# Layer 0's experts ordered on the chip by their token counts: eight with 128 slots, eight with 64 in pairs

## The chip, the core and the metric

One NeuronCore of a Trainium2 chip runs the whole program. The metric is device time of one execution in microseconds (us), lower is better. The engines are PE (matmuls, with its weight loads shown as PEld), DVE (vector), ACT (scalar), POOL and SP. SP computes nothing here: it issues the loads from device memory. A "q" behind an engine's name (SPq, ACTq) is its queue of instructions that do not compute.

## The reference, cut to what matters

Two layers; each ends in a mixture of experts over its tokens, 512 in layer 0 (256 of context, 256 latent) and 256 in layer 1. Every token goes to two of 16 experts, and each expert is a SwiGLU of width 512:

```python
probs = softmax(h @ w_router); ...
e_idx = g_idx[:, None] * EXPERTS_PER_GROUP + loc      # two experts of one group
...
return (jax.nn.silu(xblk @ w_gate[e]) * (xblk @ w_up[e])) @ w_down[e]
...
return jax.ops.segment_sum(y * weight, token)
```

`w_gate` and `w_up` are 1024 x 512 and `w_down` 512 x 1024, all float32, so one expert's weights are 6 pieces of 1.05 MB, 6.29 MB in all, and the 16 experts of a layer 100.7 MB. With the reference's inputs, expert 0 of layer 0 has 121 tokens; the other fifteen have, from most to fewest, 106, 91, 85, 81, 67, 66, 58 and then 58, 48, 47, 45, 43, 43, 38, 27.

## The kernel before

The mixture of layer 0 is the part `if full:` of `tail`. Routing leaves, for each expert, the places of its tokens in 128 slots (`place_tiles`, `indices`): `gix`, by which POOL gathers rows of the tokens from device memory (`gather`), and `six`, by which it scatters the result rows (`scatter`). `cnt` holds the counts and their maximum. Every engine loads that maximum and branches on it (`past_slots`): if some expert had more tokens than slots, `overflow` would run. With these inputs it doesn't.

Then the loop takes the experts 0 to 15 in turn. For each: eight transposes of the gathered rows (`expert_rows`, into `xh` and `xl`), the up and gate products (`expert_wide_up`, four pieces of weights), transposes of the activations (`expert_acts`), and the down product (`expert_wide_down`, two pieces). Each piece is split into a high part (`whi`, ACT, L233) and a low part (`wlo`, DVE, L234), and each product is three matmuls of 128 x 128 on 512 columns (L245 to L247). The up products of an expert stand ahead of the down product of the one before. The last two experts are not scattered; they are added through a matrix (`back_matrix`).

The pieces come through a ring of 12 tiles (`wtile`), of which the last two experts take two for their results. SP issues the loads in one written order (`Ahead.todo`); each waits until its tile has been read. A tile is free once both of its splits are done. Behind the experts' pieces SP issues six pieces of `w_ada` (L256), the scattered rows (`y<-yd`, L1742) and two more pieces of `w_ada`. PE multiplies the first `w_ada` pieces (L268), and then `combine` adds the rows (L1761).

Layer 1's mixture has 64 slots for each expert: `expert_half_up` (L1575) and `pair_down` (L1603) multiply the unsplit float32 weights, with two 64-column halves of PE side by side. The change doesn't touch it; its rows are of use below.

Of the kernel before, what the change touches and what calls it, by code (L numbers as in the profile page):

```python
# [23 lines left out]
D = 1024  # L24
# [52 lines left out]
def kernel(es, tc, A, out, dbg=None):  # L77
# [882 lines left out]

    class Ahead:


        def __init__(self, l):
            self.l = l
            self.done = {}

            up = lambda e: [(e, p) for p in range(4)]
            if l:
                down = lambda e: [(e + i, p) for p in (4, 5) for i in (0, 1)]  # L970
                self.todo = up(0) + up(1)
                for e in range(2, 16, 2):
                    self.todo += up(e) + down(e - 2) + up(e + 1)
                self.todo += down(14)
            else:
                down = lambda e: [(e, p) for p in (4, 5)]
                self.todo = up(0)
                for e in range(1, 16):
                    self.todo += up(e) + down(e - 1)
                self.todo += down(15)  # L980

        def fetch(self, n):
            for _ in range(n):
                f = self.todo.pop(0)
                self.done[f] = expert_piece(self.l, *f)
# [10 lines left out]
    def tail(l, mp, mgp, mg, side, other):  # L996
# [18 lines left out]
        with ExitStack() as ms, ExitStack() as ps_:  # L1015
# [13 lines left out]
            cnt = mo.tile([1, 17], I32, name="cnt")  # L1029
            mcol = mo.tile([128, 16 * len(rr) + 8], F32, name="mcol")  # L1030
            if full:
# [3 lines left out]
                gix = mo.tile([128, 16], U32, name="gix")  # L1035
                six = mo.tile([128, 16], U32, name="six")
# [5 lines left out]
            with ExitStack() as rs_:  # L1042
# [3 lines left out]
                if full:  # L1046
                    n2 = xg[0]
                    m34 = rp.tile([128, 2, 2, D], F32, name="m34")
                    cc = rp.tile([128, 3, 16], F32, name="cc")
                    rnb = rp.tile([128, nt, 16], BF16, name="rnb")  # L1050
# [61 lines left out]
                def tile_done(t):  # L1112
# [46 lines left out]
                    if t % 2 == 0:  # L1159
                        return  # L1160
                    weights.append(route(rp, lgs[0], t, nt, br, wts, comb, ohb, rnk, rnb if full else None, rhs, utr, one,
                                         cnt, (rows_a, rows_b) if t == nt - 1 else None))
                    if full:
                        nonlocal placed
                        placed = place_tiles(rp, (t - 1, t), cap, iot, rnb, rhs, cc, None if t < nt - 1 else
                                    lambda g: indices(rp, cc, gix, six, g))
                    if full and t == nt - 1:
                        weigh(placed)

# [22 lines left out]
                def past_slots(overflow_):  # L1192
                    mx = nc.values_load(cnt[0:1, 16:17], min_val=0, max_val=128 * nt)
# [33 lines left out]
            if full:  # L1227
                for e in range(2):
                    gather(l, xg[e], gix[:, e:e + 1], nt)
                past_slots(lambda: overflow(l, side, nt, cap, rnk, rhs, cnt))  # L1230
# [3 lines left out]
                def rows_of(e):  # L1234

                    nonlocal g
                    if e < NE:
                        rows[e] = expert_rows(ex, xg[e % 2])
                    if e + 2 < NE:
                        g = gather(l, xg[e % 2], gix[:, e + 2:e + 3], nt)  # L1240

                def acts_of(e):
                    if e >= 0:
                        acts[e] = expert_acts(ex, acts[e])

                for e in range(NE + 1):
                    if e == 0:
                        rows_of(0)
                    if e < NE:

                        with tc.issue_after(placed.ins) if e == 0 else nullcontext():
                            acts[e] = expert_wide_up(ex, e, rows.pop(e), load, lambda: acts_of(e - 1))
                    if e == 0:
                        rows_of(1)
                    if e == NE // 2:
                        m5 = [None, ex.tile([128, D], F32, name="m5")]
                        SY.dma_start(m5[1], m_dram[l][1, 5 * D:].partition_broadcast(128))
                        with tc.issue_after(g.ins):
                            back = [back_matrix(ex, i, nt, rnk, comb) for i in (NE - 2, NE - 1)]
                    if e:  # L1260
                        if e == NE:
                            acts_of(e - 1)
                        MT, ws = back[e - 1 - (NE - 2)] if e > NE - 2 else (None, None)
                        y = expert_wide_down(l, ex, e - 1, acts.pop(e - 1), six[:, e - 1:e], load, lambda: rows_of(e + 1), ws)
# [21 lines left out]
    def route(rp, lg, t1, NT_, br, wts, comb, ohb, rnk, rnb, rhs, utr, one, cnt, meanwhile):  # L1286
# [64 lines left out]
        if last:  # L1351
# [4 lines left out]
            V.tensor_copy(cf[:, 0:16], pc[0:1])  # L1356
            V.tensor_reduce(cf[:, 16:17], cf[:, 0:16], AX.X, ALU.max)
            V.tensor_copy(cnt, cf)
# [12 lines left out]
        return weights  # L1371

# [23 lines left out]
    def indices(mo, cc, gix, six, g):  # L1396

        e = slice(8 * g, 8 * g + 8)
        I = mo.tile([128, 8], F32, name="I", bufs=2)
        J = mo.tile([128, 8], F32, name="J", bufs=2)  # L1400
        K = mo.tile([128, 8], F32, name="K", bufs=2)

        V.scalar_tensor_tensor(I, cc[:, 1, e], 128.0, cc[:, 0, e], ALU.mult, ALU.add)
        V.tensor_scalar(J, cc[:, 2, e], 0.5, BIG, ALU.is_lt, ALU.mult)
        V.tensor_tensor(gix[:, e], I, J, ALU.add)
        V.tensor_scalar(K, J, C[:, CPID:CPID + 1], -1.0, ALU.mult, ALU.add)
        V.scalar_tensor_tensor(I, I, 2.0, cc[:, 2, e], ALU.mult, ALU.add)
        return V.tensor_tensor(six[:, e], I, K, ALU.add)
# [42 lines left out]
    def expert_piece(l, e, p):  # L1451

        if l == 0:
            r = wtile([128, 4, 512])
            if p < 4:

                loads.append(SY.dma_start(r, A[("w_gate", "w_up")[p % 2]][l, e].rearrange("(p k) n -> p k n", k=8)[
                    :, 4 * (p // 2):4 * (p // 2) + 4]))
            else:

                loads.append(SY.dma_start(r.rearrange("p (k c) n -> p k (c n)", c=2),
# [353 lines left out]
```

## Time and profile before

| | |
|---|---|
| median of three runs | 1747.82 us (1746.91 to 1748.83) |
| the profiled execution | 1750.19 us, its span 1748.4 us |
| PE busy | 1667.5 us, 95% of the span |
| DVE, ACT busy | 1034.2 us (59%), 805.2 us (46%) |
| moved by transfers | 380.03 MB, 217 GB/s on average |

Times in the trace are us from the span's start. The mixture of layer 0 lies between about 731 and 1036 us, that of layer 1 between about 1510 and 1745 us.

### The profile page before, as it was taken

Reading aid. Unit: us, or ns where it says so; the run is one execution under the profiler, and the core shown is the slowest. Engines: PE = TensorE matmul, PEld = TensorE weight load, DVE = VectorE, ACT = ScalarE, POOL = GpSimd, SP = SyncE. Lnnn points to the kernel's source line nnn. Section 1 sums busy time; section 2 is a strip of 40 time slices with the busy share of each in tenths; the row PEclk is TensorE's granted clock in tenths of the full one; section 3 lists DMA queues with packets and bytes.
Section 4 is the critical chain, followed back from the end, with each engine's and each line's share of the span. In section 5 each row is a group of like instructions: output and inputs, shape, how many; then the busy total and the mean of one; then the engine's idle time right before and its main releaser. Section 6 shows DMA issues by size and latency. Waiting matters only on the chain. (4 is left out here: it accounts for less than half of the span.)

```text
span 1748.4 us, 24188 instructions
## 1 busy us (share of the span) xinstructions
PE 1667.5 (95%) x8944; PEld 1231.4 (70%) x8945; DVE 1034.2 (59%) x1905; ACT 805.2 (46%) x1343; POOL 304.0 (17%) x322
## 2 busy tenths in 40 slices
PE   7999999999999999699999999999999999799998
PEld 4657878886677888488877766878887887443333
DVE  4328673557776345699978866578548865411101
ACT  3313432356577341288878755434446874211100
POOL 0003130412210221011131001133313202100000
PEclk9999999999999999799999999999999998899999
DMA  9895434233121473799999875422434348799996
GB/s 290 294 314 192 121 124 162 75 97 88 34 73 38 108 261 124 285 419 414 395 349 356 328 296 161 117 82 84 144 97 122 96 109 295 276 414 413 412 381 252
DMA packets 198448, 380.03 MB, mean 217 GB/s; under 512 B 33446, under 2 KB 130214, under 8 KB 176432
## 3 DMA queue, kind: packets, MB, share of 16 engines
q1 hardware_dynamic: 186384, 361.19, 58.3%
q10 hardware_dynamic: 7616, 9.43, 1.7%
q0 software_dynamic: 4320, 7.75, 1.2%
q8 instruction: 75, 1.23, 0.3%
q14 instruction: 53, 0.43, 0.1%
HBM read 370.50 MB, written 17.72 MB: 222 GB/s over the span
## 5 line engine op out<-in xcount | busy, mean ns | idle before, releaser
L234 DVE TENSOR_TENSOR wlo<-wraw,whi 128x1024 fp32r<-128x1024 f32 (+2 forms) x368 | 439.6, 1220 | 174.5 <-ACT whi L233 166.4
L233 ACT CAST whi<-wraw 128x1024 fp32r<-128x1024 f32 (+2 forms) x368 | 367.1, 1024 | 141.4 <-PE psg L246 59.4
L245 PE MATMUL psg<-hTh,whi 128*128 128x512 f32 (+1 forms) x576 | 205.6, 359 | 0.0
L246 PE MATMUL psg<-hTl,whi 128*128 128x512 f32 (+1 forms) x576 | 204.7, 356 | 0.0
L247 PE MATMUL psg<-hTh,wlo 128*128 128x512 f32 (+1 forms) x576 | 203.8, 356 | 0.0
L245 PE MATMUL psg<-whi,hTh 128*128 128x512 f32 (+1 forms) x392 | 147.8, 381 | 2.2 <-ACT hTh L379 2.1
L246 PE MATMUL psg<-wlo,hTh 128*128 128x512 f32 (+1 forms) x392 | 147.8, 378 | 0.1
L247 PE MATMUL psg<-whi,hTl 128*128 128x512 f32 (+1 forms) x392 | 146.8, 378 | 0.0
L245 PEld LDWEIGHTS psg<-hTh,whi 128*128 128x128 f32 x576 | 108.4, 188 | 20.7 <-issue 6.8
L247 PEld LDWEIGHTS psg<-hTh,wlo 128*128 128x128 f32 x576 | 108.3, 188 | 17.1 <-issue 4.4
L246 PEld LDWEIGHTS psg<-hTl,whi 128*128 128x128 f32 x576 | 108.6, 188 | 16.3 <-issue 4.0
L1575 PE MATMUL psg<-wraw,xT 128*64 128x512 f32 x512 | 113.4, 595 | 2.9 <-PEq L1194 2.8
L246 PE MATMUL psg<-wlo,xh 128*128 128x512 f32 x256 | 103.0, 402 | 2.7 <-DVE wlo L234 2.5
L245 PE MATMUL psg<-whi,xh 128*128 128x512 f32 x256 | 102.3, 400 | 1.4 <-ACT xh L1484 1.4
L247 PE MATMUL psg<-whi,xl 128*128 128x512 f32 x256 | 100.8, 395 | 0.0
L1575 PEld LDWEIGHTS psg<-wraw,xT 128*64 128x64 f32 x512 | 35.8, 137 | 74.0 <-issue 71.4
L245 PEld LDWEIGHTS psg<-whi,hTh 128*128 128x128 f32 x392 | 74.0, 189 | 19.3 <-ACT hTh L379 3.8
L247 PEld LDWEIGHTS psg<-whi,hTl 128*128 128x128 f32 x392 | 73.8, 189 | 15.3 <-issue 1.0
L246 PEld LDWEIGHTS psg<-wlo,hTh 128*128 128x128 f32 x392 | 74.1, 189 | 13.9 <-issue 0.5
L593 ACT ACTIVATE P<-P,smx 128x512 f32<-128x512 f32 (+1 forms) x96 | 62.3, 649 | 22.1 <-DVE smx L592 19.7
L842 POOL TENSOR_TENSOR mg<-mg,gates 128x512 f32<-128x512 f32 (+1 forms) x32 | 38.1, 1199 | 171.7 <-DVE gates L841 104.0
L1580 ACT ACTIVATE act<-psg 128x256 f32<-128x256 f32 x16 | 6.2, 384 | 130.8 <-PE psg L1575 107.3
(410 smaller groups left out, 3249.0 us busy)
## 6 DMA issues: line engine op xcount, KB each, us to landing
wraw<-in_w_down_dram SPq DMA_DIRECT2D x64, 1024.0 KB
wraw<-in_w_ada_dram SPq DMA_DIRECT2D x40, 1024.0 KB
wraw<-in_w_in_dram SPq DMA_DIRECT2D x144, 256.0 KB
wraw<-in_w_gate_dram SPq DMA_DIRECT2D x32, 1024.0 KB
wraw<-in_w_up_dram SPq DMA_DIRECT2D x32, 1024.0 KB
wraw<-in_w_gate_dram SPq DMA_DIRECT2D x64, 512.0 KB
wraw<-in_w_up_dram SPq DMA_DIRECT2D x64, 512.0 KB
wraw<-in_w_in_dram SPq DMA_DIRECT2D x24, 1024.0 KB
```

The source lines that it names most:

```text
L233: S.copy(hi[:, :, 0:n], r[:, 2 * j:2 * j + 2, 0:n])
L234: splits[0] = V.tensor_tensor(lo[:, :, 0:n], r[:, 2 * j:2 * j + 2, 0:n], hi.bitcast(F32)[:, :, 0:n], ALU.subtract)
L245: PE.matmul(ps, ah, bh, start=start, stop=False)
L246: PE.matmul(ps, ah, bl, start=False, stop=False)
L247: return PE.matmul(ps, al, bh, start=False, stop=stop)
L593: S.activation(flat, flat, AF.Exp, scale=-1.0, bias=m[:, 0:1], accum_out=m[:, 2:3])
L842: G.tensor_tensor(dst, dst, sg[:, i], ALU.add)
L1575: PE.matmul(pgu[64 * c:64 * c + 64, :], xT[:, 2 * p + k, o:o + 64], r[:, :, k, 256 * c:256 * c + 256], start=p == 0 and k == 0, stop=p == ...
L1580: S.activation(a, mk(pgu, 0, [[1, 2], [2, 128]]), AF.Silu)
```

## The change

**Order.** After the counts, `by_count` ranks experts 1 to 15 by their number of tokens on DVE; `in_order` permutes the places with the resulting 15 x 15 matrix. Position 0 is expert 0, positions 1 to 7 are the seven fullest: these eight have 128 slots and are computed as before. Positions 8 to 15 have 64 slots each, two of them share one gather and one scatter. `cnt` now holds the count plus 64 for these, so that the branch still compares with 128. The loop runs over 12 units.

**Pairs.** A pair's rows are transposed once (`pair_rows`), each of its experts goes through `expert_half_up` with its 64 slots, and `pair_down_rows` does both down products side by side. Nothing is split: the tile of a piece is free when its matmuls are done.

**Loads.** The expert behind a position is known only on the chip: SP loads its number from `order` into a register and uses it in the load's address. A pair's up pieces are two transfers of 0.5 MB each. `rsel` holds the selected columns that the last two units need.

```diff
+    FULL = 8
+    UNITS = [(0,), (1,), (8, 9), (2,), (3,), (10, 11), (4,), (5,), (12, 13), (6,), (7,), (14, 15)]
...
+                self.todo = ups(UNITS[0])
+                for a, b in zip(UNITS, UNITS[1:]):
+                    self.todo += ups(b) + down(a)
...
+                e = f[0]
+                if self.order is not None and e:
+                    if e not in self.at:
+                        self.at[e] = nc.values_load(self.order[0:1, e - 1:e], engines=[mybir.EngineType.SP],
+                                                    min_val=1, max_val=15)
+                    e = self.at[e]
+                self.done[f] = expert_piece(self.l, e, f[1], self.l == 1 or f[0] >= FULL)
...
+                        for i, r in enumerate((rnk, comb)):
+                            for p in range(3):
+                                pd = rp.tile([128, nt, 15], F32, name="pd", tag="h2T", bufs=2)
+                                with tc.issue_after(placed.ins):
+                                    V.tensor_tensor(pd, r[:, :, 1:16], mk(srt[2], 15 * (6, 13, 14)[p], [[0, nt], [1, 15]]),
+                                                    ALU.mult)
+                                    V.tensor_reduce(rsel[:, i, p], pd, AX.X, ALU.add)
...
+                            if len(UNITS[u]) == 1:
+                                acts[u] = expert_wide_up(ex, UNITS[u][0], rows.pop(u), load, lambda: acts_of(u - 1))
+                            else:
+                                xT, a = rows.pop(u), []
+                                for i, e in enumerate(UNITS[u]):
+                                    a.append(expert_half_up(ex, e, xT, 64 * i, load, None if i else lambda: acts_of(u - 1)))
+                                acts[u] = a
...
+    def by_count(rp, pc, cf, cnt, order, xs, Pm):
...
+        V.scalar_tensor_tensor(key, pc[:, 1:16], 16.0, C[:, CED + 1:CED + 16], ALU.mult, ALU.add)
+        V.tensor_tensor(cmp, mk(key, 0, [[0, 15], [1, 15]]), mk(key, 0, [[1, 15], [0, 15]]), ALU.is_ge)
+        V.tensor_reduce(pos, cmp, AX.X, ALU.add)
+        V.tensor_scalar(xs[:, 1:16], pos, FULL - 0.5, 64.0, ALU.is_gt, ALU.mult)
+        V.tensor_tensor(Pm, mk(C, CIOT, [[1, 15], [0, 15]]), mk(pos, 0, [[0, 15], [1, 15]]), ALU.is_equal)
+        V.tensor_tensor(cmp[0:1], Pm[0:1], mk(C[0:1], CIOT, [[0, 15], [1, 15]]), ALU.mult)
+        V.tensor_reduce(orf, cmp[0:1], AX.X, ALU.add)
+        V.tensor_copy(order, orf)
+        V.tensor_tensor(cf[:, 0:16], pc[0:1], xs[0:1], ALU.add)
...
+    def in_order(rp, cc, Pm, gix, six):
...
+        V.tensor_tensor(prod, mk(cc, 1, [[16, 3], [0, 15], [1, 15]]), mk(Pm, 0, [[0, 3], [15, 15], [1, 15]]), ALU.mult)
...
+        V.tensor_reduce(cp, prod, AX.X, ALU.add)
...
+        PE.matmul(ps[64:128], ident[:, 0:64], mk(cp, FULL, [[15, 3], [2, 4]]), start=True, stop=True, tile_position=(0, 64))
...
+        return indices(rp, cu, gix, six, 1, 11)
...
+    def pair_down_rows(l, ex, e, aT, sidx, load, between, ws=None):
...
+        for h in range(2):
+            r = [load(e + i, 4 + h) for i in range(2)]
+            for c in range(2):
+                for k in range(2):
+                    for i in range(2):
+                        PE.matmul(ps[c][64 * i:64 * i + 64, :], aT[i][:, k, 64 * h:64 * h + 64],
+                                  r[i][:, k, 512 * c:512 * c + 512], start=h + k == 0, stop=h + k == 2,
+                                  tile_position=(0, 64 * i))
```

What stands on SP at the branch, before. L1457 are up pieces of `expert_piece`, L256 a piece of `w_ada`, L1144 the rows that are gathered later, L1193 and L1194 are `past_slots`.

```order
L1457 DMA wraw<-in_w_gate_dram 128x2048
L256 DMA wraw<-in_w_ada_dram 128x2048
L1457 DMA wraw<-in_w_gate_dram 128x2048
L1457 DMA wraw<-in_w_up_dram 128x2048
L1144 DMA h2d_137<-xg_5360 128x1024
L1457 DMA wraw<-in_w_gate_dram 128x2048
L1457 DMA wraw<-in_w_up_dram 128x2048
L1193 TENSOR_LOAD cnt
L1193 ISA x2
L1457 DMA wraw<-in_w_up_dram 128x2048
L1194 COMPARE_AND_BRANCH
```

And in the change, up to the branch. L1546 are the up pieces (all four of expert 0), L1536 is a down piece, L996 the load of a number from `order`; six more such loads stand between the down piece and the branch.

```order
L1546 DMA wraw<-in_w_gate_dram 128x2048
L1165 DMA h2d_137<-xg_5364 128x1024
L1546 DMA wraw<-in_w_up_dram 128x2048
L1222 TENSOR_LOAD cnt
L1222 ISA x2
L996 TENSOR_LOAD order
L996 ISA x2
L1536 DMA wraw<-in_w_down_dram 128x2048
L996 TENSOR_LOAD order
L996 ISA x2
```

Six expert pieces stood ahead of the branch, five stand there now; behind it each load with an address from `order` has an ISA row ahead of it.

What stands on ACT at the same branch, before: L274 writes a row of the modulation back, L263 loads the next one into the same tile `mr`.

```order
L233 CAST whi<-wraw 128x1024 x4
L274 DMA m_dram_134<-mr 2x512 x4
L263 DMA mr<-in_b_ada_dram 32x512
L1193 TENSOR_LOAD cnt
L1194 COMPARE_AND_BRANCH
```

And in the change:

```order
L233 CAST whi<-wraw 128x1024 x4
L274 DMA m_dram_134<-mr 2x512
L1222 TENSOR_LOAD cnt
L1223 COMPARE_AND_BRANCH
```

Three of the four writes, and the load that waits for them, now stand behind the branch. On DVE, three of the four `wlo` splits that stood ahead of its branch stand behind it as well.

## Rows read from the trace of the kernel before

**Rows 1.** The page's part 1, busy time of each engine.

```profile
PE 1667.5 (95%) x8944; PEld 1231.4 (70%) x8945; DVE 1034.2 (59%) x1905; ACT 805.2 (46%) x1343; POOL 304.0 (17%) x322
```

**Rows 2.** Windows: engines' busy us, granted clock, DMA share, GB/s, four stretches.

```profile
740.00:820.00 80.00, 79.27 (x376) 66.27 (x375) 72.57 (x70) 66.48 (x79) 10.23 (x8) 1.00 1.02 418
820.00:890.00 70.00, 68.44 (x330) 57.01 (x328) 63.31 (x63) 58.17 (x69) 16.19 (x16) 1.00 1.00 395
900.00:1000.00 100.00, 98.16 (x455) 79.25 (x454) 87.64 (x87) 78.92 (x98) 13.53 (x10) 1.00 0.94 343
1520.00:1700.00 180.00, 173.72 (x782) 71.25 (x780) 22.02 (x47) 16.86 (x34) 0.00 (x0) 1.00 1.01 404
```

**Rows 3.** Timeline of SP's issues in layer 0's experts: start, us, count.

```profile
820.38 0.33 SPq L1457 DMA_DIRECT2D wraw<-in_w_gate_dram  x1
...
838.15 0.33 SPq L1457 DMA_DIRECT2D wraw<-in_w_gate_dram  x1
...
989.71 10.86 SPq L1461 DMA_DIRECT2D wraw<-in_w_down_dram  x4
...
1002.51 18.20 SPq L256 DMA_DIRECT2D wraw<-in_w_ada_dram  x6
```

**Rows 4.** SP's own waits, 690 to 1060: total us, times, longest.

```profile
SPq L1457 <- DVE wlo L234: 135.2, 52, 4.6
```

**Rows 5.** Groups by line, 740 to 850: count, busy us, mean ns, idle.

```profile
L234 DVE TENSOR_TENSOR wlo<-wraw,whi 128x1024 fp32r<-128x1024 f32 x73 | 87.0, 1223 | 10.1 <-ACT whi L233 8.8
L233 ACT CAST whi<-wraw 128x1024 fp32r<-128x1024 f32 x74 | 75.8, 1051 | 16.7 <-PE psg L247 11.0 <-PE psa L247 4.9 <-ACT whi L233 0.3
```

**Rows 6.** Groups by line and shape, whole span: layer 1's pairs, layer 0's row transposes.

```profile
L1575 PE MATMUL psg<-wraw,xT 128*64 128x512 f32 x512 | 113.4, 595 | 2.9 <-PEq L1194 2.8
...
L1603 PE MATMUL psg<-wraw,aT 128*64 128x512 f32 x256 | 60.4, 595 | 2.1 <-ACT act L1580 1.0 <-DVE aT L1592 1.0
...
L1483 PE MATMUL pst<-C,xg 128*128 128x128 f32 x128 | 19.0, 283 | 9.1 <-ACTq L1194 9.1
```

**Rows 7.** Timeline of layer 1: one expert's up products, and what follows them.

```profile
1577.65 7.09 PE L1575 MATMUL psg<-wraw,xT 128*64 128x512 f32 x32
...
1584.66 0.19 PEld L1424 LDWEIGHTS psg<-Mg,hh 128*128 128x128 f32 x1 [0.81 <-issue]
```

**Rows 8.** Timeline around the branch before layer 0's experts.

```profile
719.99 0.18 DVE L1391 TENSOR_TENSOR cc<-cc,psa 128x24 f32<-128x24 f32 x1 [1.18 <-PE psa L1384]
...
723.91 0.68 DVE L272 TENSOR_TENSOR mr<-mr,psd 128x512 f32<-128x512 f32 x1
...
724.62 1.16 ACTq L274 DMA_DIRECT2D m_dram<-mr  x4
...
729.51 1.22 DVE L234 TENSOR_TENSOR wlo<-wraw,whi 128x1024 fp32r<-128x1024 f32 x1
...
730.23 2.60 ACTq L263 DMA_DIRECT2D mr<-in_b_ada_dram  x2
731.73 1.57 PEld L1483 LDWEIGHTS pst<-C,xg 128*128 128x128 f32 x8 [9.14 <-ACTq L1194]
...
732.85 0.34 SPq L1457 DMA_DIRECT2D wraw<-in_w_gate_dram  x1
```

**Rows 9.** Windows at that branch, columns as in the second group.

```profile
727.00:730.00 3.00, 0.00 (x0) 0.00 (x0) 3.00 (x8) 0.00 (x0) 0.00 (x0) 0.50 0.88 347
730.00:733.00 3.00, 1.27 (x6) 1.27 (x7) 0.73 (x1) 0.00 (x0) 0.00 (x0) 0.50 0.16 57
```

**Rows 10.** Line L1193, the load of `cnt`, on SP: ns min/median/max.

```profile
L1193 SPq TENSOR_LOAD <-cnt x2: 286/377/468, 719.2 to 1684.3; - x2
L1193 SPq FUSED_REGOPS  x2: 172/176/181, 719.7 to 1684.6; - x2
```

**Rows 11.** The page's part 3: POOL's queue of gathers and scatters.

```profile
q0 software_dynamic: 4320, 7.75, 1.2%
```

**Rows 12.** Timeline of PE behind the last expert.

```profile
1036.30 5.36 PE L268 MATMUL psd<-wraw,cT 128*32 128x512 f32 x48
...
1041.58 1.13 PE L1761 MATMUL psa<-y,dg 128*128 128x512 f32 x2
```

More of the change, by code (lines that the diff above doesn't have):

```diff
@@ L966, in __init__ @@
             self.done = {}
+            self.order, self.at = None, {}
             up = lambda e: [(e, p) for p in range(4)]
@@ L1034, in tail @@
                     G.memset(rhs[:, t, 1], float(t))
-                gix = mo.tile([128, 16], U32, name="gix")
-                six = mo.tile([128, 16], U32, name="six")
+                gix = mo.tile([128, 12], U32, name="gix")
+                six = mo.tile([128, 12], U32, name="six")
+                order = mo.tile([1, 15], I32, name="order")
+                xs = mo.tile([128, 16], F32, name="xs")
+                G.memset(xs[:, 0:1], 0.0)
+                rsel = mo.tile([128, 2, 3, nt], F32, name="rsel")
                 xg = [mo.tile([128, D], F32, name=f"xg{i}") for i in range(2)]
@@ L1049, in tail @@
                     cc = rp.tile([128, 3, 16], F32, name="cc")
+                    srt = order, xs, rp.tile([128, 15, 15], F32, name="Pm")
                     rnb = rp.tile([128, nt, 16], BF16, name="rnb")
@@ L1227, in tail @@
             if full:
-                for e in range(2):
-                    gather(l, xg[e], gix[:, e:e + 1], nt)
-                past_slots(lambda: overflow(l, side, nt, cap, rnk, rhs, cnt))
+                col = lambda u: slice(u[0], u[0] + 1) if u[0] < FULL else slice(FULL + (u[0] - FULL) // 2, FULL + (u[0] - FULL) // 2 + 1)
+                NU = len(UNITS)
+                for u in range(2):
+                    gather(l, xg[u], gix[:, col(UNITS[u])], nt)
+                past_slots(lambda: overflow(l, side, nt, cap, rnk, rhs, cnt, xs))
@@ L1231, in tail, with rows_of @@
+                ahead.order = order
                 ex = ms.enter_context(tc.tile_pool(name=f"ex{l}", bufs=1, side=side))
                 ys, rows, acts, g = [], {}, {}, None
-                def rows_of(e):
+                def rows_of(u):
                     nonlocal g
[L1237 to L1244, printed above, removed]
@@ L1246, in tail @@
-                for e in range(NE + 1):
-                    if e == 0:
-                        rows_of(0)
[L1249 to L1253, printed above, removed]
+                    if u < NU:
+                        rows[u] = (expert_rows if len(UNITS[u]) == 1 else pair_rows)(ex, xg[u % 2])
+                    if u + 2 < NU:
+                        g = gather(l, xg[u % 2], gix[:, col(UNITS[u + 2])], nt)
@@ new lines, in acts_of @@
+                def acts_of(u):
+                    if u >= 0:
+                        acts[u] = (expert_acts if len(UNITS[u]) == 1 else pair_acts)(ex, acts[u])
+                for u in range(NU + 1):
+                    if u == 0:
+                        rows_of(0)
+                    if u < NU:
+                        with tc.issue_after(placed.ins) if u == 0 else nullcontext():
+                            if len(UNITS[u]) == 1:
[5 more added lines that the diff above has]
+                                acts[u] = a
+                    if u == 0:
@@ L1258, in tail @@
                         with tc.issue_after(g.ins):
[L1259 to L1264, printed above, removed]
+                            back = [back_matrix(ex, p, nt, rsel) for p in ((0,), (1, 2))]
+                    if u:
+                        if u == NU:
+                            acts_of(u - 1)
+                        MT, ws = back[u - 1 - (NU - 2)] if u > NU - 2 else (None, None)
+                        c = col(UNITS[u - 1])
+                        down = expert_wide_down if len(UNITS[u - 1]) == 1 else pair_down_rows
+                        y = down(l, ex, UNITS[u - 1][0], acts.pop(u - 1), six[:, c], load, lambda: rows_of(u + 1), ws)
                         if MT is not None:
@@ L1566, in expert_xT, with expert_half_up @@
         return xT
-    def expert_half_up(ex, e, xT, o, load):
+    def expert_half_up(ex, e, xT, o, load, between=None):
         pgu = ps_g()
@@ L1577, in expert_half_up @@
                               start=p == 0 and k == 0, stop=p == 3 and k == 1, tile_position=(0, 64 * c))
+            if p == 1 and between:
+                between()
         a = ex.tile([128, 2, 128], F32, name="act", tag="act", bufs=2)
```

157 lines of the change are left out of this document (99 added, 58 removed).

## Prediction

> **What bounds the kernel now.** I read the page's busy times first: PE is busy 95% of the span [rows 1], so nearly every stage looks bound by PE, and an average can't say more. The order of both programs is the same outside layer 0's mixture and the few us on either side, so the windows over that stage come next. Between 740 and 820 us three things are full at once: PE 79 of 80 us, the transfers at a DMA share of 1.02 and 418 GB/s, and DVE 73 of 80 us [rows 2]. Later the share stays near 1 while the rate falls to 395 and then 343 GB/s [rows 2].
>
> Which of them ends last? SP's own waits name it: 52 times SP waits with the next load until a low-part split has freed a tile [rows 4]. So the ring of 12 tiles is full, and transfers wait for PE, DVE and ACT, not the other way round. Splits alone cost DVE 87 and ACT 76 of 110 us [rows 5]. An expert takes 838.15 - 820.38 = 17.8 us from issue to issue [rows 3]. The transfers have little in reserve, though: 6.29 MB of weights and about 0.5 MB of rows in and out per expert, at 418 GB/s, is 16.2 us. **The gain can therefore not be read from PE: it ends where the transfers become the bound.**
>
> **PE's side of the change.** An expert with 64 slots costs 7.09 us for its up products (113.4 us for 16 experts, [rows 6]; one of them as a piece of the timeline, [rows 7]). A pair's down products cost 60.4 / 8 = 7.6 us [rows 6], its eight row transposes 19.0 / 16 = 1.2 us [rows 6], and four transposes of activations about half of that. A pair: 2 x 7.09 + 7.6 + 1.8 = 23.6 us, against 2 x 17.8 = 35.6 before. Leaving a run of side-by-side matmuls adds something: after such a run the next load of weights has 0.81 us of "issue" ahead of it [rows 7]. The new order leaves such runs some five to nine times per pair, 4 to 7 us if each costs that, nothing if the transposes cover it; I take 28 us for a pair, 23.6 and 31 as the ends. Eight single experts at 17.8 and four pairs at 28 are 254 us, plus some 2 us for the slow clock at the start (0.50 in [rows 9]). Splits fall by half on DVE and ACT, so neither limits PE.
>
> **The start of the stage.** This is lengthened. `by_count` adds five operations of 225 elements per row and four small ones to DVE, `in_order` two of 675, two copies, and a round trip over PE; `rsel` adds twelve of 60. None of these widths is in the trace. Bounds: 0.18 us (24 elements) and 0.68 us (512) for the first, 0.68 and 1.22 (1024) for the two wide ones [rows 8]. By width I take 0.4 and 0.9 us, and 0.15 for the rest: 2.6 + 2.7 + 1.8 = 7.1 us, bounds 4 and 10. Against this, three splits of 1.22 us move behind the branch, -3.7 us, and DVE has idle time between the placings (1.18 us before 719.99, [rows 8]) that takes up about 1. ACT reaches the branch last today: its four small writes begin at 724.62, it then waits until 730.23 to reload the tile they read, and PE's first transposes start 1.5 us later, at 731.73 [rows 8]. That wait moves behind the branch. So DVE, now at 730.7 (729.51 + 1.22), arrives at about 733.5 and is the last, and PE and SP restart about **3 us later** (bounds 0 and 6): SP's first load at 736 instead of 732.85 [rows 8]. Behind the branch ACT's wait for that write-back lies ahead of some splits; four `whi` halves done earlier cover it, and if they didn't, PE would lose at most the 4 us that ACT waits now.
>
> The seven loads of numbers from `order` on SP before the branch cost 0.29 to 0.47 us each plus 0.17 [rows 10], under 5 us, while SP stands at the branch for 12 us anyway; the later eight are hidden behind tiles that aren't free. If they weren't, 0.65 us each. The transfers have run dry by then: the share falls from 0.88 to 0.16 in the last 3 us before the restart [rows 9]. Five expert pieces stand ahead of the branch instead of six, so one more MB falls behind it.
>
> **The transfers' side, which sets the end.** Behind the branch there are 91 of 96 pieces, 95.4 MB; about 7 MB of gathered and scattered rows (7.75 in all, [rows 11], less the first two gathers; fewer slots move no fewer rows, since empty ones move nothing); 0.5 MB of modulation. Together 102.9 MB. The rate: 418 GB/s where the ring has just been refilled, 404 for layer 1's 0.5 MB halves [rows 2]. I take 412, nearer to the first, because layer 1's stretch ends in a thinner stream. 736 + 102.9 / 0.412 = 736 + 250 = 986 us for the last piece. PE by itself would end at 735 + 256 = 991. Both together, with each waiting now and then for the other, about 993, against 1036.3 [rows 12].
>
> Then comes the tail. Today PE multiplies six `w_ada` pieces (5.4 us) and starts to combine at 1041.58 [rows 12]; those pieces were loaded behind the experts' last ones, from 1002.51 [rows 3], while PE was still 34 us from its end. In the change the stream reaches them no sooner than 986: six pieces and the first 1 MB of rows are 7.3 MB, 18 us, and 2 us until they are used, so combining starts at 986 + 20 = **1006 us**. PE, at 993 + 5.4, waits for that: a part of the gain on the experts is left in the tail. From there the order of work is the old one, and layer 1 follows with the transfers under half busy.
>
> **Sum:** 1041.6 - 1006 = 35.6 us, about 35. The profiled execution took 1750.19 us, 1.8 more than its span and 2.4 above the median of the runs; taken off the median, 1747.8 - 35 gives **1713 us**.
>
> **Dynamic addresses.** Each load from unit 1 on takes its address from a register. No such load runs in the trace. Lower bound: SP's issue of 0.33 us [rows 3]. Upper: with a register operation of 0.17 [rows 10] and a second such load, about 1. There are 122 behind the branch in 250 us, one every 2.0 us, so either end is hidden; I take nothing.
>
> **One rule weighed.** Between 740 and 820 us this core moved 418 GB/s for 80 us [rows 2]. The Trainium skill (DMA: Bandwidth & Descriptors, Specifications) gives about 358 GB/s as the limit of device memory for one core and 435 GB/s for the fabric. By the first, 736 + 102.9 / 0.358 + 22 would be about 1046 us, later than today's 1041.6; the trace disagrees with it in this very stage, and only the second is compatible with it.
>
> **Rivals.**
> 1. *The transfers were the bound already.* A share of 0.94 to 1.02 throughout [rows 2] speaks for it; SP's waits for splits [rows 4] and 418 GB/s under the same mixture speak against it. At the mean of the three windows, 380 GB/s: 736 + 271 + 21 = 1028, a gain of 14 and 1734 us.
> 2. *PE stays the bound.* If changes of form cost the full price and the transposes cover nothing, a pair takes 31 us and PE ends near 1003; with waits for pieces 1010, combining at 1016: 25 us less, 1723. The row of 0.81 us speaks for it; that the ring holds two experts ahead, against it.
> 3. *Slower.* If 0.5 MB halves, register addresses and rows together hold the transfers at the rate of 900 to 1000, 343 GB/s [rows 2], the last piece lands at 736 + 300 = 1036 and combining starts at 1060: 18 us more, 1766. It decides below 110.2 MB / 303.6 us = 363 GB/s, the rate at which 736 + time + 2 reaches today's 1041.6. The fall to 343 speaks for it; that SP was then waiting for tiles, and layer 1's 404 from halves of the same size, against.
> 4. *It doesn't do what it says*: an expert beyond its slots would bring `overflow`, with 6.3 MB loaded and used in small steps for each, over 16 us apiece. The counts (121 and 106 of 128, 58 of 64) speak against it.
> 5. *More than forecast*: branch not delayed (733), 421 GB/s, PE at 23.6 per pair: combining at 733 + 244 + 19 = 996, 45 us less, 1702.
>
> **Chances.** The forecast with what lies around it, gains of 25 to 42 us, 0.60; rival 5 and beyond 0.09; rival 1, gains of 8 to 25, 0.13; rival 2 0.07; rival 3 0.07, where I count also issue costs of over 2.3 us per load, by which SP would come to the same; rival 4 0.01; the remaining 0.03 no change. The range from 1701 to 1737 leaves out about 2 in 10: half of rival 5, a quarter of rival 1, and all of the last three. A measurement here tells 0.2%, 3.5 us, from no change: faster 0.89, same 0.03, slower 0.08.
>
> **What the changed profile would show.** Right: windows between 760 and 980 at a share near 1.0 and over 400 GB/s to the end, SP's waits no longer on splits but on nothing longer than a piece, PE with short idle stretches in the pairs that end with a transfer, the last down piece issued before 975, combining at about 1006 with PE waiting for `w_ada` or rows ahead of it; PE's first transposes at 733 to 737; 7.1 us per expert of a pair. Wrong: SP busy with issues while tiles are free (addresses), idle "issue" of several us in each pair (changes of form), a share of 1.0 at under 380 GB/s (rival 1), a clock under 1.0 in the pairs, which would double their PE time, or lines of `overflow` at work.

## The result, and the profile of the changed kernel

The changed kernel takes 1734.12 us (median of 5 runs, 1730.52 to 1738.66), the kernel before 1748.83 beside it: a ratio of 0.9916, 95% interval 0.9896 to 0.9937, 14.7 us less. The forecast was 1713 us, 35 less. The sign and the range (1701 to 1737) held; the gain is 0.42 of the forecast one.

Part 1 of the changed kernel's page, which answers to [rows 1], says as little as before: PE is busy 94%.

```profile
PE 1625.5 (94%) x8714; PEld 1144.1 (66%) x8715; DVE 917.1 (53%) x1818; ACT 696.0 (40%) x1223; POOL 287.6 (17%) x319
```

Windows over the stage, columns as in [rows 2]:

```profile
740.00:820.00 80.00, 76.95 (x345) 49.92 (x344) 47.05 (x51) 43.03 (x55) 10.27 (x9) 0.99 1.02 410
820.00:890.00 70.00, 64.38 (x287) 40.00 (x287) 33.01 (x35) 28.93 (x38) 15.52 (x21) 0.98 1.01 410
900.00:1000.00 100.00, 93.45 (x402) 56.04 (x403) 48.81 (x50) 43.64 (x56) 5.51 (x5) 0.98 0.96 375
```

DVE falls from 73 to 47 us in the first window, as it should. PE now has gaps, and the transfers are full until 890 us and fall to 375 GB/s after 900. Read alone, that would be rival 1. The waits say otherwise. SP's own waits, first from 760 to 900, then from 912 to 995 us (total us, times, longest), the answer to [rows 4]:

```profile
SPq L1542 <- DMA wraw<-in_w_gate_dram: 16.8, 12, 2.2
SPq L1536 <- DMA wraw<-in_w_down_dram: 16.1, 8, 3.2
```

```profile
SPq L1536 <- DVE wlo L234: 18.0, 5, 6.8
SPq L1536 <- PE psg L1644: 12.5, 7, 3.3
SPq L1546 <- DVE wlo L234: 9.4, 4, 3.2
```

At first SP waits mostly for earlier loads to land (the stream is full); from 912 on it waits for a split or a product to free a tile, as in the kernel before. What PE itself waits for, 738 to 1020 us, has no transfer among its eleven rows:

```profile
PE pst L1557 <- DVEq L1223: 8.5, 1, 8.5
PE pst L1671 <- DVE act L1652: 5.6, 6, 0.9
PE psg L245 <- ACT whi L233: 4.2, 3, 1.6
PE psg L246 <- DVE wlo L234: 3.0, 4, 1.0
PE pst L1617 <- POOL M L1615: 2.4, 3, 1.4
PE psa L246 <- DVE wlo L234: 1.6, 3, 0.5
PE psa L1685 <- ACT aT L1673: 1.2, 1, 1.2
...
```

The first row is the branch. Without it PE waits 20.1 us for ACT, DVE and POOL; in the kernel before, the same list has 6.8, and 9.1 more for the branch. Nor are these waits transfers at one remove: in the same stretch the splits on ACT and DVE waited for a piece once each.

```profile
ACT whi L233 <- DMA wraw<-in_w_down_dram: 0.8, 1, 0.8
DVE wlo L234 <- DMA wraw<-in_w_down_dram: 0.5, 1, 0.5
```

The ends of the stage on SP and PE, which answer to [rows 8] and [rows 12]:

```profile
736.13 0.37 SPq L1546 DMA_DIRECT2D wraw<-in_w_gate_dram  x1
```

```profile
737.80 1.95 PE L1557 MATMUL pst<-C,xg 128*128 128x128 f32 x8 [8.49 <-DVEq L1223]
...
1012.35 7.11 PE L1685 MATMUL psa<-wraw,aT 128*64 128x512 f32 x32 [1.22 <-ACT aT L1673]
1019.39 5.36 PE L268 MATMUL psd<-wraw,cT 128*32 128x512 f32 x48
1024.68 1.12 PE L1882 MATMUL psa<-y,dg 128*128 128x512 f32 x2
```

SP restarts at 736.13, as forecast; PE at 737.8 (733 to 737 forecast, 731.7 before); its experts end at 1019.4 (993 forecast, 1036.3 before), and combining follows directly at 1024.7 (1006 forecast, 1041.6 before). It starts 16.9 us earlier than before; the spans of the two profiled executions differ by 18.9 us, the medians by 14.7.

PE's 281.6 us between 737.8 and 1019.4 can be split with the groups by line of that stretch:

```profile
L1644 PE MATMUL psg<-wraw,xT 128*64 128x512 f32 x256 | 57.8, 597 | 0.0
L1685 PE MATMUL psa<-wraw,aT 128*64 128x512 f32 x128 | 36.8, 602 | 1.2 <-ACT aT L1673 1.2
L1661 PE MATMUL pst<-C,xg 128*128 128x128 f32 x32 | 5.0, 285 | 0.0
L1671 PE MATMUL pst<-C,act 128*128 128x128 f32 x16 | 3.4, 293 | 5.6 <-DVE act L1652 5.6
L1620 PE MATMUL psd<-rsel,M 128*64 128x1 f32 (+1 forms) x24 | 2.4, 220 | 0.8 <-POOL M L1615 0.8
L1617 PE MATMUL pst<-C,M 128*128 128x128 f32 x8 | 1.9, 293 | 2.4 <-POOL M L1615 2.4
```

With the idle time ahead of them the pairs' four lines are 57.8 + 36.8 + 5.0 + 3.4 + 5.6 + 1.2 = 109.8 us, **27.5 per pair** (28 forecast). The last two lines, the matrices for combining, are 7.5. What remains, 281.6 - 109.8 - 7.5 = 164.3, is eight single experts: **20.5 each**, where the forecast had 17.8.

### The profile page after: what moved, and what is told of

It reads as the page before. It is cut to its first block, busy times and chain, and to the rows that moved or that the text cites. A ratio compares the mean times of both kernels' runs of the same rounds, so it can differ in the third digit from the quotient of the medians.

```text
span 1729.5 us, 23727 instructions
## 1 busy us (share of the span) xinstructions
PE 1625.5 (94%) x8714; PEld 1144.1 (66%) x8715; DVE 917.1 (53%) x1818; ACT 696.0 (40%) x1223; POOL 287.6 (17%) x319
## 5 line engine op out<-in xcount | busy, mean ns | idle before, releaser
L234 DVE TENSOR_TENSOR wlo<-wraw,whi 128x1024 fp32r<-128x1024 f32 (+2 forms) x272 | 325.2, 1217 | 172.7 <-ACT whi L233 166.6
L233 ACT CAST whi<-wraw 128x1024 fp32r<-128x1024 f32 (+2 forms) x272 | 269.0, 1012 | 128.6 <-PE psg L246 59.4
L1644 PE MATMUL psg<-wraw,xT 128*64 128x512 f32 x768 | 172.9, 601 | 2.6 <-PEq L1223 2.6
L1644 PEld LDWEIGHTS psg<-wraw,xT 128*64 128x64 f32 x768 | 53.5, 138 | 106.6 <-issue 102.7
L1652 DVE TENSOR_TENSOR act<-act,psg 128x256 f32<-128x256 f32 x24 | 10.1, 420 | 121.7 <-ACT act L1651 121.7
L593 ACT ACTIVATE P<-P,smx 128x512 f32<-128x512 f32 (+1 forms) x96 | 62.1, 648 | 22.2 <-DVE smx L592 19.8
L302 POOL TENSOR_TENSOR hrs<-hrs,nhalf 128x8 f32<-128x8 f32 (+1 forms) x28 | 44.1, 1577 | 111.2 <-DVE hrs L301 111.1
L1724 PE MATMUL psg<-wraw,aT 128*64 128x512 f32 x256 | 60.4, 595 | 2.1 <-ACT act L1651 1.0
```

Of the source, the lines that this page charges most:

```text
L233: S.copy(hi[:, :, 0:n], r[:, 2 * j:2 * j + 2, 0:n])
L234: splits[0] = V.tensor_tensor(lo[:, :, 0:n], r[:, 2 * j:2 * j + 2, 0:n], hi.bitcast(F32)[:, :, 0:n], ALU.subtract)
L302: return G.tensor_tensor(dst, dst, nhalf[:, 0:dst.shape[-1]], ALU.pow)
L593: S.activation(flat, flat, AF.Exp, scale=-1.0, bias=m[:, 0:1], accum_out=m[:, 2:3])
L1644: PE.matmul(pgu[64 * c:64 * c + 64, :], xT[:, 2 * p + k, o:o + 64], r[:, :, k, 256 * c:256 * c + 256], start=p == 0 and k == 0, stop=p == ...
L1652: V.tensor_tensor(a, a, mk(pgu, 256, [[1, 2], [2, 128]]), ALU.mult)
```

## The experiments

All ratios are to the kernel before, run beside on the same chip; the last three columns are us in the profile of each (PE's restart behind the branch, the end of the experts on PE, the start of combining).

| kernel | ratio, 95% interval | restart | experts end | combining |
|---|---|---|---|---|
| changed | 0.9916, 0.9896 to 0.9937 | 737.8 | 1019.4 | 1024.7 |
| less_loads | 0.9804, 0.9773 to 0.9835 | 734.3 | 998.8 | 1004.1 |
| half_up | 0.9779, 0.9746 to 0.9812 | 734.4 | 997.8 | 1010.4 |
| presplit | 0.9884, 0.9852 to 0.9916 | 736.8 | 1017.8 | 1023.1 |
| static | 0.9842, 0.9808 to 0.9877 | 735.3 | 1008.4 | 1013.6 |
| later_acts | 0.9822, 0.9795 to 0.9848 | 736.1 | 1009.7 | 1015.0 |
| later_static | 0.9877, 0.9848 to 0.9907 | 737.7 | 1016.2 | 1021.5 |
| pre_later | 0.9828, 0.9800 to 0.9856 | 737.1 | 1004.1 | 1012.9 |
| later_less | 0.9780, 0.9753 to 0.9806 | 734.1 | 993.0 | 998.3 |
| pairs_late | 0.9829, 0.9812 to 0.9847 | 742.1 | 1012.0 | 1019.4 |
| all_single | 1.0099, 1.0066 to 1.0132 | 739.5 | 1056.4 | 1061.7 |
| pad | 0.9884, 0.9859 to 0.9909 | 735.3 | 1016.3 | 1021.6 |
| before_shift | 1.0026, 1.0010 to 1.0041 | 734.4 | 1041.6 | 1046.9 |
| all_single_pad | 1.0057, 1.0036 to 1.0077 | 730.6 | 1043.8 | 1049.1 |
| later_pad | 0.9832, 0.9811 to 0.9852 | 741.0 | 1011.9 | 1017.3 |
| late_best | 0.9825, 0.9804 to 0.9845 | 737.5 | 1001.5 | 1014.7 |
| best2 | 0.9860, 0.9841 to 0.9878 | 739.7 | 1004.8 | 1005.5 |

Theory T says that the transfers bound the changed kernel (rival 1, whose 1734 us is the measured time); theory P that PE still does, with its waits for ACT and DVE (rival 2, of which only 1723 was expected).

**Less to load, less to multiply.**

```diff
+            r = [load(e, 4 + h)] * 2                  # less_loads
-            for k in range(2):
+            for k in range(1):                        # half_up, in expert_half_up
```

> Of each pair the down pieces of its second expert are not loaded; the first expert's are used for both (that part of the output is wrong). Transfers fall by 8 of 96 pieces, 8.4 MB, while PE, DVE and ACT do the same work. Theory T (the transfers at about 395 GB/s are the bound of the changed kernel): 8.4 / 0.395 = 21 us less, about 1713 us, combining starts near 1004. Theory P (PE, its instructions and its waits for ACT and DVE, is still the bound): the stage ends within 4 us of before, combining at 1021 to 1026, about 1732 us, and SP's waits move from landed transfers to tiles that aren't free.

> The up products of the eight paired experts take only half of the 1024 rows of the weights: 128 of 256 matmuls are left out (that part of the output is wrong), 8 x 3.55 = 28 us of PE; all pieces are still loaded. Theory P: faster by what the transfers then allow: at 412 GB/s the last piece lands near 988 and combining starts near 1008 instead of 1024.7, 15 to 20 us less, about 1717 us; PE then waits for pieces in the pairs. Theory T: no gain, within 4 us of 1734.

half_up is 24 us faster than the changed kernel by the ratios (0.9916 - 0.9779 of 1750), against T. Not all of that is this stage: layer 1 uses `expert_half_up` too, so 256 of its 512 products are left out as well, which the expectation overlooked. In the profiles combining starts 14.3 us earlier, and 7.5 us are gained behind it; the experts' stretch is 18.2 us shorter. T had no gain. But less_loads is 20 us faster, which T had foretold and P had not. Its trace shows why this doesn't decide for T: with fewer loads the scheduler also gave PE another order. The pairs' down products, whose runs in the changed kernel are broken seven times by transposes of other units, are broken twice:

```profile
L1685 PE MATMUL psa<-wraw,aT 128*64 128x512 f32 x128 | 28.8, 597 | 1.2 <-ACT aT L1673 1.2
```

That is 8.0 us less for the same products; PE's waits fall from 20 to 13, and it restarts 3.5 us earlier: 18.6 of the 20.6 us by which combining starts earlier in the profile. The edit changed two things, so it settles nothing by itself. half_up keeps the seven breaks and the 36.8 us, and shows what the transfers can do. Its windows and its tail on PE:

```profile
740.00:820.00 80.00, 75.65 (x336) 51.58 (x335) 51.25 (x53) 47.88 (x59) 8.96 (x8) 1.00 1.02 411
820.00:890.00 70.00, 61.24 (x255) 35.70 (x254) 29.96 (x34) 29.41 (x40) 16.70 (x22) 0.93 1.01 411
900.00:1000.00 100.00, 89.36 (x380) 52.66 (x378) 48.79 (x52) 43.41 (x58) 5.52 (x5) 0.97 1.01 411
```

```profile
997.83 2.13 PE L268 MATMUL psd<-wraw,cT 128*32 128x512 f32 x16
1001.39 1.06 PE L268 MATMUL psd<-wraw,cT 128*32 128x512 f32 x8 [1.43 <-DMA wraw<-in_w_ada_dram]
...
1010.41 1.13 PE L1882 MATMUL psa<-y,dg 128*128 128x512 f32 x2
```

With less for PE to do the same mixture of transfers moves 411 GB/s to the end of the stage, so the 375 of the changed kernel is tiles that come late, not a limit of the transfers. And here is the tail that the forecast described: PE waits for `w_ada` pieces, four times.

**Registers, or order?** In static SP loads experts 0 to 15 by fixed numbers (`ahead.order = None`); in later_static the same upon later_acts, which pins more of PE's order (the numbers are still loaded into registers there).

> The numbers of the order are still computed, but SP loads the experts by the fixed numbers 0 to 15, without registers (so tokens meet the wrong weights). The work is otherwise the same. If addresses from registers cost anything on the path: faster, by up to 122 x 0.4 = 49 us if each load's issue were on it. Theories P and T both: within 3 us of 1734, SP issues in 0.33 us as before, since SP waits between nearly all of its loads.

> As later_acts, but SP loads the experts by fixed numbers; the numbers of the order are still loaded into registers and not used (tokens meet the wrong weights). PE's order in the pairs is that of later_acts but for a few transposes, which was not so for the earlier kernel with fixed numbers. If the 12 us that the earlier one gained came from its order on PE: within 4 us of later_acts. If register addresses cost them: 10 us or more below later_acts.

static is 13 us faster than the changed kernel, later_static 10 us slower than later_acts. Registers can't do both. In the changed kernel's trace an issue by register takes 0.33 us like any other [rows 3]; here are the pairs' loads of `w_gate` (ns min/median/max), 32 of the 122:

```profile
L1542 SPq DMA_DIRECT2D wraw<-in_w_gate_dram x32: 332/333/341, 744.2 to 972.2; - x32
```

What differs in both is the scheduler's order: in static the pairs' down products are broken six times and take 34.9 us, in later_static a few products stand elsewhere. That the order alone makes the 13 and the 10 us is not shown: PE's restart also moved, by 2.5 us down and 1.6 up.

**The order on PE and ACT.** presplit issues the next single expert's splits ahead of the copies of the pair's output; later_acts lets transposes of activations follow the next expert's first 24 products; pre_later does both.

```diff
+        for p in range(2):                             # presplit, pair_down_rows
+            pre[then, p] = split_raw(load(then, p))
+        with tc.issue_after(splits[1].ins):
             return put(l, y, ps, sidx, ws)
...
-                between()
+                with tc.issue_after(last.ins):         # later_acts, expert_wide_up
+                    between()
```

> Nothing is left out. Three times the splits of a single expert's first two pieces stand on ACT behind the copies of the pair's output, which wait for the pair's last down product; here those splits are issued ahead of the two copies. PE's order is untouched. Theory P with ACT's order as a part of the price: the waits of 0.98 + 1.04, 1.62 + 0.76 and 1.62 + 0.76 us and most of the clock's fall to 0.83 behind them go, 6 to 10 us less than the changed kernel, about 1726 us. Theory T: no gain, within 3 us of 1734.

> Nothing is left out. The transposes of a unit's activations may be issued on PE only behind the first 24 up products of the single expert that follows, so that in PE's order the pairs' down products are no longer broken by another expert's transposes, and a single expert's cast of activations no longer stands on ACT between the pair's down product and the next splits. Theory P, in the form that the eight single experts beside the pairs and the broken runs carry the missing gain: the 36 us of the pairs' down products fall towards 30, the 10 us of PE's waits ahead of products of splits are halved, 5.6 us of waits for activations mostly go: 10 to 18 us less than the changed kernel, combining at 1007 to 1015, about 1720 us. Theory T: within 4 us of 1734.

> Nothing is left out. Both edits: the activations' transposes later, and the next single expert's first splits ahead of the copies of the pair's output. If the splits were still blocked in the earlier kernel because the cast of activations, which waits for the pair's last down product, stood ahead of them: 2 to 5 us less than later_acts, and the waits of PE ahead of a single expert's first products are gone. If the splits don't matter: the same as later_acts.

> As later_acts, with the down pieces of each pair's second expert not loaded, 8.4 MB less (that part of the output is wrong); PE's order is nearly that of later_acts. Theory P: within 5 us of later_acts. Theory T, or transfers that have become the bound once PE's order is mended: 10 to 20 us less than later_acts.

presplit brought 5.6 us by the ratios (its interval overlaps the changed kernel's), just under the 6 to 10: in the profile the experts' stretch is only 0.6 us shorter. The reason is on ACT in the changed kernel, at the end of the third pair:

```profile
959.87 0.58 ACT L1662 COPY xT<-pst 128x512 f32<-128x512 f32 x1 [6.96 <-PE pst L1661]
964.23 0.58 ACT L1696 COPY y<-psa 128x512 f32<-128x512 f32 x1 [3.78 <-PE psa L1685]
965.10 0.58 ACT L1585 CAST ah<-pst 128x512 fp32r<-128x512 f32 x1 [0.29 <-PE psa L1685]
965.94 0.59 ACT L1696 COPY y<-psa 128x512 f32<-128x512 f32 x1 [0.26 <-PE psa L1685]
966.43 4.94 ACT L233 CAST whi<-wraw 128x1024 fp32r<-128x1024 f32 x5
```

ACT idles for 10.7 us, and then copies and splits all come at once; PE waits 1.62 us for the first of these splits. The cast `ah` also waits for the pair's down products: `pair_acts` puts `aT` in the buffer of `ah`, so the cast may not write before the last of them has read it. In presplit that cast still stood ahead of the splits. later_acts moves it: 1719.65 us, 16 us faster than the changed kernel by the ratios, inside what P had said. In the profiles combining starts 9.7 us earlier, and it is the pairs that gain: their down products take 31.2 us, and the transposes of their activations wait 1.9 us instead of 5.6.

```profile
L1686 PE MATMUL psa<-wraw,aT 128*64 128x512 f32 x128 | 31.2, 600 | 1.2 <-ACT aT L1674 1.2
```

PE's waits for splits and casts, which P had halved, rose from 10.1 to 13.4 us. pre_later then ends the experts on PE 5.6 us earlier than later_acts: the waits ahead of single experts' first products, for `whi` and `wlo`, fall from 8.1 us to 1.0. But the time is the same:

```profile
1004.10 3.64 PE L268 MATMUL psd<-wraw,cT 128*32 128x512 f32 x32
1009.07 1.07 PE L268 MATMUL psd<-wraw,cT 128*32 128x512 f32 x8 [1.33 <-DMA wraw<-in_w_ada_dram]
1011.55 1.06 PE L268 MATMUL psd<-wraw,cT 128*32 128x512 f32 x8 [1.42 <-DMA wraw<-in_w_ada_dram]
1012.94 1.10 PE L1892 MATMUL psa<-y,dg 128*128 128x512 f32 x2 [0.32 <-DMA y<-yd]
```

In this tail PE has reached the transfers: it waits for `w_ada` and for rows. later_less is 7 us faster than later_acts by the ratios (the intervals just overlap), between what P and T gave; PE's waits fell there too, so this one doesn't settle how much of it was the transfers.

**Where the singles stand.** pairs_late changes only `UNITS`.

> Only the list of units is changed: seven single experts, three pairs in a row, the last single expert, the last pair (nothing is left out). Theory P, with the extra cost of the single experts due to their neighbours: the waits ahead of a single expert's first products come once instead of three times, some 6 us less; against this, three pairs in a row take more from the stream (6 x 6.29 MB at 411 GB/s is 92 us, PE 81 us), which the full ring of two experts covers in part: between 6 us less and 4 us more than the changed kernel. Theory T: the order of the units makes no difference to the bytes, within 3 us of 1734.

It is 15 us faster than the changed kernel by the ratios (its profile is of its slowest run, 1728.4 of 1716.0 to 1728.4), more than expected. Even in that run the experts' stretch is 269.9 us long instead of 281.6. With one step from a pair to a single expert in place of three, the same units cost PE 12 us less: 6 of it in the pairs (28.8 us for the down products), the rest in the single experts.

**Ordering alone, and the place in memory.** all_single orders the experts but gives all 16 their 128 slots (`FULL = 16`). pad, before_shift and all_single_pad add one unused tile:

```diff
                 ex = ms.enter_context(tc.tile_pool(name=f"ex{l}", bufs=1, side=side))
+                pad = ex.tile([128, 8], F32, name="pad")
+                G.memset(pad, 0.0)
```

> The experts are ordered by their counts and loaded by register, but all 16 have 128 slots and go alone; nothing is left out. It shows what the ordering alone costs. Theory P: start 5 to 6 us later, the 7 ns per product on 1152 products 8 us, together 10 to 14 us slower than the kernel before, about 1760 us; so the pairs themselves give back some 26. If register addresses cost issue time: SP issues of over 0.33 us and more than 20 us slower.

> The changed kernel with an unused tile of 32 bytes ahead of the experts' tiles; nothing is left out, and every engine's order is the same. In the changed kernel those tiles (the transposed rows and activations that are loaded as weights) lie 224 bytes further on than before, and from the first expert on its full-width products follow each other every 234 ns instead of 227. If the place in memory is the cause: 227 ns again with the 32 bytes, 576 x 7 ns = 4 us less, about 1730 us. If not: 234 ns and the same time.

> The kernel before, with an unused tile of 32 bytes ahead of the experts' tiles, so that they lie where a single expert's products took 234 ns in the changed kernel (a multiple of 64 bytes); nothing is left out and every engine's order is the same. If the place alone sets the pace: 234 ns instead of 227 in the stage, 1152 x 7 ns = 8 us slower, a ratio near 1.005. If it needs the new code: 227 ns and the same time.

> All 16 experts single and ordered on the chip, with the 32 bytes. If the 17 us that ordering alone cost are the later start (7.8 us at PE's restart), the pace of 1152 products (8 us) and little else: 8 us less than without the 32 bytes, a ratio near 1.005, about 1757 us. If the pace is of no account for the time: 1.010 again.

Ordering alone makes the kernel 1.0% slower, 17 us. The pairs then save 17 + 14.7 = 32 us, 8.0 each; the forecast had 35.6 - 28 = 7.6. The pace follows the place. The changed kernel, and the changed kernel with 32 bytes, each in its first expert's neighbour:

```profile
760.50 0.39 PE L246 MATMUL psg<-wlo,xh 128*128 128x512 f32 x1
760.73 0.40 PE L247 MATMUL psg<-whi,xl 128*128 128x512 f32 x1
760.97 0.40 PE L245 MATMUL psg<-whi,xh 128*128 128x512 f32 x1
```

```profile
760.41 0.39 PE L246 MATMUL psg<-wlo,xh 128*128 128x512 f32 x1
760.63 0.39 PE L247 MATMUL psg<-whi,xl 128*128 128x512 f32 x1
760.86 0.39 PE L245 MATMUL psg<-whi,xh 128*128 128x512 f32 x1
```

234 ns from start to start and 227 (medians over the stage), and 234 for the kernel before when it is shifted. The means (of distances under 260 ns) lie 5 ns apart, not 7. In time the shift costs the kernel before 4.6 us of the 8 expected, and the 32 bytes give all_single 7.4 back; pad is 5.6 us faster than the changed kernel by the ratios, but the experts' stretch in its profile only 0.6 us shorter. In later_pad it is 2.7 us shorter than in later_acts, but PE restarts 4.9 us later there, and the whole is no faster. Of the 17 us, 7 are thus the pace; the other 10 are not split further. PE's restart varies too much: 730.6 to 742.1 in the 16 profiles with the sorting (median 737.0), against 731.7 and 734.4 without.

**How far it goes.** later_pad, late_best (pairs_late, later_acts and the 32 bytes) and best2 (pre_later, the 32 bytes, and `w_ada` loaded behind the first rows).

> The changed kernel with the activations' transposes later and the 32 bytes; nothing is left out. 576 x 7 ns = 4 us less than with the transposes alone, a ratio of 0.980, about 1716 us, if PE still is the bound there; the same 0.982 if the transfers have become it.

> Seven single experts, three pairs in a row, the last single, the last pair; with the activations' transposes later and the 32 bytes; nothing is left out. Each of the three edits alone took 4 to 15 us off the changed kernel. If they add up: about 1708 us. If the transfers bind in the three pairs in a row (92 us for their 37.7 MB): no better than 1716 us, the share near 1.0 at 410 GB/s between 880 and 1000 us.

> Nothing is left out: the activations' transposes later, the next splits ahead of the pair's copies, the 32 bytes, and the six pieces of modulation weights loaded behind the first rows for combining instead of ahead of them. With the first two edits PE ended the experts at 1004 and then waited for transfers, combining at 1012.9. If that tail is now the bound, as the forecast had it: combining directly behind the experts, at 1000 to 1006, 5 to 10 us less than with the two edits alone, about 1712 us. If not: within 3 us of 1720.

The edits don't add up: later_acts, pre_later, pairs_late, later_pad and late_best all lie at 0.982 to 0.983, some 31 us below the kernel before. In late_best the transfers are full to the end, at 416 GB/s:

```profile
900.00:1000.00 100.00, 91.64 (x414) 42.58 (x412) 22.97 (x29) 22.56 (x35) 3.98 (x4) 0.98 1.02 416
```

Its experts end at 1001.5, and PE then waits 5.2 us for five `w_ada` pieces; combining starts at 1014.7. pre_later and pairs_late wait for transfers there too, 3.1 and 1.7 us. In later_acts and later_pad no transfer stands among PE's waits, and combining follows the experts at once; so that all five meet a floor of the transfers is not shown, only that pairs_late, which is one line, and later_acts each come as far alone as any of them. best2 does start combining at 1005.5, as hoped, but the products with `w_ada` then fall between combining's and layer 1's first ones, and the whole is no faster than pre_later (0.9860 against 0.9828).

## Why the prediction was wrong, step by step

- **The price of a single expert: the step that failed.** "Eight single experts at 17.8" took the distance between two issues in the best stretch of the kernel before [rows 3] for all of them. That kernel's own stage contradicts it: 1036.3 - 731.7 = 304.6 us is 19.0 per expert. Both ends stand in [rows 8, 12]. In the changed kernel a single costs 20.5, so the eight cost 164 us where the sum has 142. PE was to end the experts at 991 and ended at 1019.4, 28 us later: 22 are this term, 7.5 the matrices for combining, for which the sum had no term, 2.8 the later restart; the pairs and the slow clock at the start, for which 2 us had been added, give 4 back.
- **Where the 2.7 us per single expert come from**, by the same split of each profile: 18.6 in the kernel before, 19.4 in all_single (no pair in it, the slower pace), 20.5 in the changed kernel, 20.9 in later_acts, 20.1 in pre_later, 19.8 in pairs_late. So 0.8 is the wrong stretch, 0.8 comes with the ordering alone, and 1.1 with the pairs as neighbours: PE waits 10.1 us for splits, casts and copies, where half of the 5.2 before would be 2.6. pre_later and pairs_late take a part of it back; later_acts gains in the pairs (27.5 to 25.2 us each), not here. Each price is from one profile, and what makes up the second 0.8 beside the pace stays open.
- **The accounts.** Before, the matrices for combining cost 6.8 us by the same two groups, and (304.6 - 6.8) / 16 = 18.6 is an expert's share, 148.9 for eight. The pairs save 148.9 - 109.8 = 39.1; the singles lose 164.3 - 148.9 = 15.4, the matrices 0.7, the restart 6.1. That leaves 16.9, by which combining starts earlier.
- **The pair at 28 us** was right (27.5), its waits included: some 0.9 us before six of the eight runs of `L1671`, and 36.8 us instead of 30 for the down products. Of the 3.9 over the bare 23.6, the broken down products are 1.7, where the forecast had 4 to 7 for changes of form, and the waits for activations, which it did not name, are 1.4: that the size fits is in part luck.
- **The start** 3 us later (bounds 0 and 6): SP's first load 3.3 us later, as forecast; PE 6.1 in this profile, just over its upper bound, and 3 to 5 by the median of the 16. DVE's last split ahead of the branch ended at 735.7 (733.5 forecast), and ACT reached the branch at 735.5, since its write of a modulation row waits for `L272`, which DVE now does at 733.75.
- **The transfers' side, which sets the end:** wrong for this kernel, where SP issued the last down piece at 993 (975 forecast) and PE, none of whose products waited for a piece, ended 26 us later; right in its rate. 412 GB/s was forecast, 411 to 416 is measured in half_up and late_best. The Trainium skill (DMA: Bandwidth & Descriptors, Specifications) puts the limit of device memory at about 358 GB/s per core, a stack's 716 divided by two cores; half_up's 411 over 100 us, on one core, lies above it again, and below its 435 GB/s for the fabric.
- **The tail** that waits for `w_ada`: not in the changed kernel, where combining follows the experts at once; present in half_up, pre_later and late_best, where PE ends at 997.8 to 1004.1, and short (1.7 us) in pairs_late. In the two kernels with fewer loads PE ends at 998.8 and 993.0, and combining follows at once.
- **Registers and overflow** at nothing: right, by the issues of 0.33 us and with no line of `overflow` in the trace. **Rival 1** had the time (1734) with the wrong mechanism: a transfer share of 1.0 and SP's waits for landings showed a full queue, while no transfer stands among PE's waits: its hit is luck. **Rival 2** had the mechanism, PE, at 1723: its size was off by the singles, which it too had at 17.8, and by the matrices.

## What to carry to other kernels

Price a unit of work by the whole stage divided by its count, not by its best stretch, and check that units times price gives the stage that is there. A transfer share of 1.0 says that the queue is full, not that anybody waits: look for a transfer among the waits of the engine that ends last, and of those it waits for. When units of two kinds alternate, look at what their outputs stand ahead of on the other engines' queues, and at buffers that the kinds share; and when an experiment goes through a scheduler, compare the two orders before its time is believed, since here an order alone (later_acts, pairs_late) was worth some 15 us. When an edit is in a function, ask who else calls it.

## What the runs showed of the hardware that was not expected

The pace of full-width products depended on where the tile that is loaded as weights lies: 227 ns with the experts' tiles (`xh`, `xl`, `ah`, `al`) at an address of 32 modulo 64 bytes, 234 at a multiple of 64 (medians), in either kernel and with the same order of instructions. Only these two places were tried. The split halves (`whi`, `wlo`) lie at 32 modulo 64 in all four programs, so whether the place counts or its relation to theirs was not separated.
